# Modulation sums and narrow projections of a three-layer mixer network as fp32 products on column tiles

## The chip, the cores and the metric

The kernel runs on one core of a Trainium2 chip. The metric is the device time of one launch in microseconds; before the change its median over three runs is 2794.69 us (2786.75 to 2796.12).

## What is computed

A sequence of 512 tokens with 1024 features passes through one block of a first kind and two blocks of a second kind, in fp32. Each block starts by turning one conditioning row `c` into six rows of 1024 numbers (shift, scale and gate, once for the mixer and once for the feed-forward network):

```python
c_act = jax.nn.silu(c)
mod = c_act @ w_ada[l] + b_ada[l]          # 1024 -> 6 * 1024
sh1, sc1, g1, sh2, sc2, g2 = split(mod, 6)
h = rmsnorm(x, gain) * (1.0 + sc1) + sh1
proj = h @ w_in[l]                         # wide, with some narrow parts at its end
x = x + g1 * (mixer(proj) @ w_out[l])
h = rmsnorm(x, gain2) * (1.0 + sc2) + sh2
x = x + g2 * ((silu(h @ w_gate) * (h @ w_up)) @ w_down)
```

In the first block the mixer joins dilated attention (8 heads) and a gated delta rule (8 heads). The delta rule takes two gate logits per head, which are 16 of the columns of `w_in`. In the second kind the mixer joins three gated linear attentions. One of them takes its decays from a projection of rank 2 x 16, which is 32 of the columns of `w_in`. The output is one more RMS norm.

## The kernel before

Activations lie with the features on the partitions: `h` is 8 tiles of 128 x 512. To keep fp32 accuracy at the speed of the `fp32r` type, every weight strip and every activation is split into a high and a low part (`split`, L103 on ScalarE and L104 on VectorE). Each product is then made three times (`mm3`, L123 to L125: high x high, high x low, low x high). A projection (`proj`) loads one strip of 1024 x 128 weights, splits it, and issues 8 x 3 products of 512 columns. A product whose operands are plain fp32 shows as two records in the trace.

The order of work is written out by hand. A list `Dense` holds the projections with a cost for each; the mixer's own chains (delta rule, attention) call `d.fill(us)` at points where TensorE (PE) would stand, and so many projections are issued there. A second list, `extra`, rides on it: each step of the projections' list calls `extra.fill(0.6)`, and the mixer calls it at some further points. `extra.need("gate")` forces it up to a mark ahead of the state recurrence, and `extra.rest()` runs what is left after it. Within this order the compiler's scheduler may issue an instruction earlier when its engine has nothing else ready. Each engine then runs its queue in order. All weight loads are issued by one queue, SP.

The late part of the first block's modulation (the last four of its six rows, eight groups of 512 numbers) is `extra` of the first mixer (`ada_list(0, range(2, 6))`, then `ada`). For each group eight tiles `araw` of 128 x 512 weights are loaded (L311, two buffers). VectorE multiplies each by a column of `c_act` and adds it into `acc` (L313, L315), so that `acc` holds 128 partial sums per number. `ada_sum` adds up the partitions with one product whose weights are a single column (L333), ScalarE copies the row out (L334), and a DMA stores it in DRAM (`mods`, L335). `ada_load` and `ada_rows` bring the rows back as columns (a load, a transpose at L348, a VectorE add). A mark (`self.mark`, with `issue_after`) keeps VectorE's adds behind certain instructions of the mixer.

The modulations of the second and third block are `extra` of the feed-forward networks of the blocks before them (`ada_list(1 or 2, range(6))`). The sums are alike, with loads of 1 MB. Each finished `acc` is split into high and low parts and added up by two `fp32r` products with one column. Their groups are summed one at a time.

Two narrow projections use `proj` with few columns. `gates` (in `mixer1`) has 16 columns and is transposed by four small products (L620). `lr_in` (in `mixer2`, once per layer) has 32, and `c_decay` multiplies its rows by `wal` (L1254).

The first groups of the first modulation (`ada_first`) already use products on column tiles: L395 has weights of 32 columns, in `cz` one real column beside zeros, and `tile_position` puts four of them side by side. `mrow` is the copied row (L406), and L409 turns it into columns by products whose moving operand is one column of ones.

Of the kernel before, what the change touches and what calls it, by code (L numbers as in the profile page):

```python
# [30 lines left out]
def cap(ap, off, dims):  # L31
    return bass.AP(ap.tensor, ap.offset + off, [list(ap.ap[0])] + [list(d) for d in dims])
# [37 lines left out]
class Net:  # L70
    def __init__(self, ctx, tc, A, out, dbg=None):
        self.stages = self.mark = None
# [60 lines left out]
    def proj(self, w, act, kn, n=P, zero=None, tag="mm"):  # L133

        W = self.strip(w, kn, n, zero)
        ps = (self.mm if tag == "mm" else self.mx)()
        for k in range(kn):
            self.mm3(ps[:n], (W[0][:, k], W[1][:, k]), act(k), k == 0, k == kn - 1)
        return ps

# [70 lines left out]
    def setup(self):  # L211
# [4 lines left out]
        nc.gpsimd.memset(self.one, 1.0)  # L216
        self.scr = cp.tile([P, 1], F32, name="scr")
        self.mean = cp.tile([P, 1], F32, name="mean")
        nc.gpsimd.memset(self.mean, 1.0 / D)
# [3 lines left out]
        nc.sync.dma_start(out=crow, in_=A["c"].rearrange("a (r f) -> (a r) f", f=P))  # L223
        self.ident = self.const("c_ident", [P, P])
        self.lm = cp.tile([P, 160], U8, name="lm")
        self.xd = self.dp.tile([2, P, 4 * T], F32, name="xd")
# [34 lines left out]
    def setup2(self):  # L261
# [27 lines left out]
        self.lb, self.olb = lb, olb  # L289

    def ada(self, li, g, part):

        nc = self.nc
        w = self.A["w_ada"][0] if li == 0 else self.A["w_ada_2"][li - 1]
        cs = self.cs[min(li, 1)]
        if part == 0:
            if self.sums:
                self.ada_sum()
            self.acc = self.wp.tile([P, T], F32, name="acc", tag="acc", bufs=2)
        acc = self.acc  # L300
        n = 4 if li else 2
        if li:
            raws = self.t8("araw")
            nc.sync.dma_start(out=raws, in_=w[n * part * P:n * (part + 1) * P, T * g:T * g + T].rearrange("(k p) f -> p k f", p=P))
        with self.tc.issue_after(self.mark.ins) if self.mark else nullcontext():
            for k in range(n * part, n * (part + 1)):
                if li:
                    raw = raws[:, k % n]
                else:
                    raw = self.wp.tile([P, T], F32, name="araw", tag="araw", bufs=2)  # L310
                    nc.sync.dma_start(out=raw, in_=w[k * P:(k + 1) * P, T * g:T * g + T])  # L311
                if k == 0:
                    nc.vector.tensor_scalar(out=acc, in0=raw, scalar1=cs[:, 0:1], scalar2=None, op0=ALU.mult)  # L313
                else:
                    nc.vector.scalar_tensor_tensor(out=acc, in0=raw, scalar=cs[:, k:k + 1], in1=acc,  # L315
                                                   op0=ALU.mult, op1=ALU.add)
        if n * (part + 1) == KT:
            parts = [acc]
            if li:
                t = self.t8("ada", F32R)  # L320
                parts = [t[:, 0], t[:, 1]]
                self.split(parts[0], parts[1], acc)
            self.sums.append((li, g, parts))
# [12 lines left out]

# [244 lines left out]
    def mixer1(self, extra, norm):  # L581
# [148 lines left out]
        def delta_pairs(t):  # L730
# [16 lines left out]
            for e in range(2):  # L747
                h = 2 * t + e
                nt = self.t2("nt")
                v.tensor_tensor(out=nt, in0=ps[0][e], in1=gbs[e], op=ALU.mult)  # L750
                nc.gpsimd.dma_start(out=nts[4 * h:4 * h + 4].rearrange("t (j i) -> j t i", j=P), in_=four(nt))
                last = v.tensor_tensor(out=four(noff[h // 4][:, h % 4]), in0=four(nt), in1=mask(off), op=ALU.mult)
                v.tensor_tensor(out=qkm[h // 4][:, h % 4], in0=ps[1][e], in1=gbs[e], op=ALU.mult)
            if t == 1:
                self.mark = last

# [164 lines left out]
        def attend(h):  # L921
# [19 lines left out]
            for i in range(4):  # L941
                w = (i + 1) * P
                self.mark = v.tensor_scalar(out=pr[:, i, :w], in0=pr[:, i, :w], scalar1=sm[:, 8 + i:9 + i], scalar2=None,
                                            op0=ALU.mult)
# [12 lines left out]
            if e == 1:  # L957
                o = self.t2("oa")
                self.mark = v.tensor_copy(out=back(o), in_=pv[t])
                self.split(y[0][0][:, t], y[0][1][:, t], o)  # L960
# [242 lines left out]
    def mixer2(self, l, norm):  # L1203
# [31 lines left out]
        def lr_in():  # L1235
            wal = self.t2("wal")
            nc.gpsimd.memset(wal[:32], 0.0)
            for n in range(2):
                nc.sync.dma_start(out=wal[16 * n:16 * n + 16, 256 * n:256 * n + 256], in_=A["w_alpha_2"][l, n])
            ps = self.proj(W[:, 5632:5664], H, KT, n=32)  # L1240
            lr = self.t2("lr")
            nc.scalar.copy(out=lr[:32], in_=ps[:32])
# [286 lines left out]

    def ada_list(self, li, groups):  # L1530
        d = Dense()
        for g in groups:
            n = 2 if li else 4
            for i in range(2 * n):
                d.add("ada", 1.8 / n, lambda g=g, i=i: self.ada(li, 2 * g + i // n, i % n))
                if g == 3 and i == 0:
                    d.add("gate", 0.4, lambda: self.ada_rows(li, groups[0], 3))
            if g in (2, 5):
                d.add("ada", 0.4, self.ada_sum)
                d.add("ada", 0.4, lambda g0=max(g - 2, groups[0]), g1=g + 1: self.ada_load(li, g0, g1))  # L1540
        d.add("ada", 0.4, lambda: self.ada_rows(li, 3, 6))
        return d

    def run(self):
# [10 lines left out]
        mods = lambda li, i: (self.gain[li][:, 8 * i:8 * i + 8], self.mod[li][:, 24 * i:24 * i + 8])  # L1555
        self.mixer1(self.ada_list(0, range(2, 6)), self.norm(*mods(0, 1)))
        self.ffn(0, A["w_gate"][0], A["w_up"][0], A["w_down"][0], self.between, gained=True, extra=self.ada_list(1, range(6)))
        each, final = self.final_parts()
        for l in range(2):
            self.mixer2(l, self.norm(*mods(1 + l, 1)))  # L1560
            wf = A["w_ffn_in_2"][l]
            self.ffn(1 + l, wf[:, :2816], wf[:, 2816:], A["w_ffn_out_2"][l], final if l else self.norm(*mods(2, 0)),
                     extra=None if l else self.ada_list(2, range(6)), each=each if l else None)
        for _ in self.stages:
# [63 lines left out]
```

## Time and profile before

| | |
|---|---|
| median of three runs | 2794.69 us |
| the profiled execution's own time | 2791.13 us |
| its span, first to last instruction | 2789.3 us |
| PE busy | 2713.4 us (97%) |
| DVE (VectorE) busy | 1717.7 us (62%) |
| ACT (ScalarE) busy | 1173.5 us (42%) |
| mean granted TensorE clock | 0.990 |

The first mixer lies from about 60 to 435 us after the span's start, the first feed-forward network from there to about 800. PE means TensorE's matmuls, PEld its weight loads, DVE VectorE, ACT ScalarE, POOL GpSimd, SP the queue of the loads. "L333" is line 333 of the kernel. A matmul's record includes the time in which its results run out of the array, so records overlap; distances from start to start show how fast they follow each other.

### The profile page before, as it was taken

The numbers are of one execution on the slowest core, as the hardware profiler recorded it, in microseconds if no ns is written. First come the engines' busy times: TensorE is split into PE (matmuls) and PEld (weight loads), VectorE is DVE, ScalarE is ACT, GpSimd is POOL, SyncE is SP. The second block draws the span as 40 slices with busy tenths as digits, with TensorE's granted clock in tenths as the row PEclk, the third lists the DMA queues.
The fourth block names the chain that finished last, engine by engine and source line by source line (L and its number), as shares of the span: only waits on it lengthen the run. The fifth ranks groups of instructions, "written<-read, shape, count | busy, mean of one in ns | idle before, by whom it ended". The sixth has DMA issues, their size and how long they took to land.

```text
span 2789.3 us, 42619 instructions
## 1 busy us (share of the span) xinstructions
PE 2713.4 (97%) x17518; PEld 2202.2 (79%) x17518; DVE 1717.7 (62%) x2690; ACT 1173.5 (42%) x1799; POOL 41.7 (1%) x79
## 2 busy tenths in 40 slices
PE   8999999999999999999999999989999999999998
PEld 4786678888887787887888888877877878888887
DVE  4777756747378777757466573567777665533334
ACT  4643334222255655445343232465554453422223
POOL 0011000000000000100000000000000000000000
PEclk8999999999999999999999999999999999999999
DMA  7454534646232222332446463322223334333332
GB/s 262 135 148 121 148 123 151 219 151 219 85 107 70 62 81 69 104 104 72 136 129 233 143 228 94 105 62 69 70 75 91 101 85 131 89 99 98 96 94 83
DMA packets 471314, 330.65 MB, mean 119 GB/s; under 512 B 15447, under 2 KB 426223, under 8 KB 469584
## 3 DMA queue, kind: packets, MB, share of 16 engines
q1 hardware_dynamic: 468176, 320.51, 37.9%
q0 software_dynamic: 2944, 7.43, 0.9%
q8 instruction: 137, 2.24, 0.3%
q14 instruction: 57, 0.47, 0.1%
HBM read 312.55 MB, written 13.24 MB: 117 GB/s over the span
## 4 chain that ended last, share of the span: by engine, by line
PE 84%; DVE 5%; ACT 5%; DMA 3%; issue 2%; SPq 1%; POOL 0%; DVEq 0%; ACTq 0%; POOLq 0%
PE mm L123 21%; PE mm L124 21%; PE mm L125 21%; PE mx L124 2%; PE mx L123 2%; PE mx L125 2%; PE mm L201 2%; PE mm L203 2%; PE mm L202 2%; DMA araw<-in_w_ada_dram 1%; PE mx L1120 1%; ACT whi L103 1%; PE mx L131 1%; DVE S L104 1%; DVE wlo L104 1%
## 5 line engine op out<-in xcount | busy, mean ns | idle before, releaser
L123 PE MATMUL mm<-hh,whi 128*128 128x512 f32 (+1 forms) x2248 | 864.9, 388 | 13.8 <-ACT hh L495 9.0
L103 ACT CAST whi<-raw 128x1024 fp32r<-128x1024 f32 (+2 forms) x451 | 438.8, 974 | 1042.6 <-PE mm L124 737.9
L124 PE MATMUL mm<-hl,whi 128*128 128x512 f32 (+1 forms) x2248 | 868.4, 387 | 1.7 <-DVE hl L496 1.2
L125 PE MATMUL mm<-hh,wlo 128*128 128x512 f32 (+1 forms) x2248 | 867.1, 386 | 0.0
L104 DVE TENSOR_TENSOR wlo<-raw,whi 128x1024 fp32r<-128x1024 f32 (+2 forms) x451 | 507.2, 1126 | 364.3 <-ACT whi L103 343.0
L123 PEld LDWEIGHTS mm<-hh,whi 128*128 128x128 f32 x2248 | 421.1, 189 | 108.8 <-ACT hh L495 12.8
L124 PEld LDWEIGHTS mm<-hl,whi 128*128 128x128 f32 x2248 | 424.0, 189 | 88.8 <-DVE hl L496 4.6
L125 PEld LDWEIGHTS mm<-hh,wlo 128*128 128x128 f32 x2248 | 424.1, 189 | 87.6 <-issue 3.8
L124 PE MATMUL mm<-hid,whi 128*128 128x512 f32 (+1 forms) x564 | 212.5, 377 | 0.0
L123 PE MATMUL mm<-hid,whi 128*128 128x512 f32 (+1 forms) x564 | 212.3, 376 | 0.0
L125 PE MATMUL mm<-hid,wlo 128*128 128x512 f32 (+1 forms) x564 | 211.9, 376 | 0.0
L500 DVE SCALAR_TENSOR_TENSOR x<-mm,mod,x 128x512 f32<-128x512 f32 (+1 forms) x116 | 80.4, 694 | 178.0 <-PE mm L125 176.5
L315 DVE SCALAR_TENSOR_TENSOR acc<-araw,cs,acc 128x512 f32<-128x512 f32 x224 | 167.9, 749 | 19.0 <-DMA araw<-in_w_ada_dram 14.4
L550 DVE TENSOR_TENSOR sg<-mm,sg 128x512 f32<-128x512 f32 x66 | 45.6, 690 | 147.9 <-PE mm L125 146.0
L1176 DVE TENSOR_TENSOR R<-R,tot 128x512 f32<-128x512 f32 x192 | 126.4, 685 | 6.6 <-PE mx L1141 5.1
L201 PE MATMUL mm<-whi,hh 128*128 128x256 f32 x448 | 129.5, 289 | 0.0
L203 PE MATMUL mm<-whi,hl 128*128 128x256 f32 x448 | 129.2, 288 | 0.0
L202 PE MATMUL mm<-wlo,hh 128*128 128x256 f32 x448 | 128.8, 287 | 0.1
L123 PEld LDWEIGHTS mm<-hid,whi 128*128 128x128 f32 x564 | 106.1, 188 | 20.4 <-issue 1.2
L125 PEld LDWEIGHTS mm<-hid,wlo 128*128 128x128 f32 x564 | 106.1, 188 | 19.2
L124 PEld LDWEIGHTS mm<-hid,whi 128*128 128x128 f32 x564 | 106.1, 188 | 19.2
L454 DVE RECIPROCAL rstd<-rstd 128x512 f32<-128x512 f32 x24 | 80.4, 3351 | 13.4 <-ACT rstd L453 13.4
(377 smaller groups left out, 3375.7 us busy)
## 6 DMA issues: line engine op xcount, KB each, us to landing
raw<-in_w_in_dram SPq DMA_DIRECT2D x164, 512.0 KB
araw<-in_w_ada_dram SPq DMA_DIRECT2D x48, 1024.0 KB
raw<-in_w_ffn_in_dram SPq DMA_DIRECT2D x88, 512.0 KB
araw<-in_w_ada_dram SPq DMA_DIRECT2D x64, 256.0 KB
raw<-in_w_ffn_out_dram SPq DMA_DIRECT2D x32, 512.0 KB
raw<-in_w_gate_dram SPq DMA_DIRECT2D x22, 512.0 KB
raw<-in_w_up_dram SPq DMA_DIRECT2D x22, 512.0 KB
raw<-in_w_ada_dram SPq DMA_DIRECT2D x16, 512.0 KB
```

Of the source, the lines that this page charges most:

```text
L103: self.nc.scalar.copy(out=hi, in_=src)
L104: self.nc.vector.tensor_tensor(out=lo, in0=src, in1=hi.bitcast(F32), op=ALU.subtract)
L123: m(out=ps, lhsT=w[0], rhs=a[0], start=first, stop=False)
L124: m(out=ps, lhsT=w[0], rhs=a[1], start=False, stop=False)
L125: return m(out=ps, lhsT=w[1], rhs=a[0], start=False, stop=last)
L201: m(out=o, lhsT=a[0][:, sl], rhs=hi[:, k % 4], start=k == 0, stop=False)
L202: m(out=o, lhsT=a[0][:, sl], rhs=lo[:, k % 4], start=False, stop=False)
L203: m(out=o, lhsT=a[1][:, sl], rhs=hi[:, k % 4], start=False, stop=k == KT - 1)
L315: nc.vector.scalar_tensor_tensor(out=acc, in0=raw, scalar=cs[:, k:k + 1], in1=acc, op0=ALU.mult, op1=ALU.add)
L454: nc.vector.reciprocal(out=r, in_=r)
L500: self.nc.vector.scalar_tensor_tensor(out=self.x(f)[:, sl], in0=ps[:, sl], scalar=g[:, f:f + 1], in1=self.x(f)[:, sl], op0=ALU.mult, op1=A ...
L1176: v.tensor_tensor(out=o, in0=o, in1=half(1 - c), op=ALU.mult)
```

## The change

The late modulation of the first block is done in 16 steps, two for each group. A step (`ada_late`, `ada_raw`, `ada_mm`, `ada_cols`) loads four tiles of weights into four buffers and multiplies each by its column of `c_act`, repeated 32 times by a stride of 0. The four fp32 products stand side by side on the four column tiles. A step copies the result (128 x 512, four sums, each on 32 partitions) to `arow`. One step later it makes columns of it: four fp32 products with the moving column `four1`, which has ones at rows 0, 32, 64 and 96 and zeros elsewhere, and one add into `mod`. The rows no longer go through DRAM. The mark is gone.

The later modulations keep VectorE's sums. Up to four finished sums wait in one tile `accs` and are added up together, by fp32 products on four column tiles, without a split. Their rows are loaded and transposed once per block, not twice.

The narrow projections (`narrow`) use the unsplit weights: 16 fp32 products in four sets of four column tiles, each tile with a quarter of the contraction, for the high and the low part of `h`. The four partial results are added by the product that follows: in `gates` by a selecting matrix `sel`, in `lr_in` by four copies of `wal` on 128 rows.

```diff
+    def narrow(self, w, act):
+        raw = self.t2("wn")[:, :KT * 32].rearrange("p (k f) -> p k f", k=KT)
+        self.nc.sync.dma_start(out=raw, in_=w.rearrange("(k p) f -> p k f", p=P))
+        ps = self.mm()
+        for i in range(2):
+            for k in range(2):
+                for b in range(4):
+                    self.nc.tensor.matmul(out=ps[32 * b:32 * b + 32], lhsT=raw[:, 4 * k + b], rhs=act(4 * k + b)[i].bitcast(F32),
+                                          start=i + k == 0, stop=i + k == 2, tile_position=(0, 32 * b))
+        return ps
...
+    def ada_raw(self, g, part):
+        w = self.A["w_ada"][0]
+        raws = []
+        for k in range(4 * part, 4 * part + 4):
+            raws.append(self.wp.tile([P, T], F32, name="araw", tag="araw", bufs=4))
+            self.nc.sync.dma_start(out=raws[-1], in_=w[k * P:(k + 1) * P, T * g:T * g + T])
+        self.araw = raws
+
+    def ada_mm(self, part):
+        nc = self.nc
+        ps = self.mx()
+        for b in range(4):
+            nc.tensor.matmul(out=ps[32 * b:32 * b + 32], lhsT=cap(self.cs[0], 4 * part + b, [[0, 32]]), rhs=self.araw[b],
+                             start=True, stop=True, tile_position=(0, 32 * b))
+        self.arow = self.t2("arow")
+        nc.scalar.copy(out=self.arow, in_=ps)
+
+    def ada_cols(self, g, part):
+        nc = self.nc
+        pc = self.mx()
+        for j in range(4):
+            nc.tensor.matmul(out=pc[:, j:j + 1], lhsT=self.arow[:, j * P:(j + 1) * P], rhs=self.four1, start=True, stop=True)
+        c = slice(4 * g, 4 * g + 4)
+        mod = self.mod[0]
+        nc.vector.tensor_tensor(out=mod[:, c], in0=pc[:, :4], in1=(mod if part else self.V[0])[:, c], op=ALU.add)
+        if part and g == 9:
+            self.ada_gain(0, 4, slice(0, KT))
...
     def ada_sum(self):
...
-        li, g, parts = self.sums.pop()
         ps = self.mx()
         row = self.t2("row")
-        ones = self.mean128[:, 0:1] if li else self.mean
-        for i, a in enumerate(parts):
-            nc.tensor.matmul(out=ps[0:1], lhsT=ones, rhs=a, start=i == 0, stop=i == len(parts) - 1)
-        nc.scalar.mul(out=row[0:1], in_=ps[0:1], mul=float(P if li else D))
-        nc.sync.dma_start(out=self.mods[li][g:g + 1], in_=row[0:1])
+        n = len(self.sums)
+        for j, (li, g, acc) in enumerate(self.sums):
+            nc.tensor.matmul(out=ps[32 * j:32 * j + 32], lhsT=cap(self.one, 0, [[0, 32]]), rhs=acc, start=True, stop=True,
+                             tile_position=(0, 32 * j))
+        nc.scalar.copy(out=row[:32 * n], in_=ps[:32 * n])
+        for j, (li, g, acc) in enumerate(self.sums):
+            nc.sync.dma_start(out=self.mods[li][g:g + 1], in_=row[32 * j:32 * j + 1])
+        self.sums = []
...
         def gates():
-            ps = self.proj(W[:, 3584:3600], self.hact, KT, n=16)
+            ps = self.narrow(W[:, 3568:3600], self.hact)
             g = self.t2("g")
-            nc.scalar.copy(out=g[:16], in_=ps[:16])
+            nc.scalar.copy(out=g, in_=ps)
+            sel = consts[:, 448:464]
+            v.tensor_tensor(out=sel, in0=i64[:, 16:32], in1=i64[:, 48:64], op=ALU.add)
             pt = self.mx()
             for t in range(4):
-                nc.tensor.transpose(out=pt[:, 16 * t:16 * t + 16], in_=g[:16, t * P:(t + 1) * P], identity=self.ident[:16, :16])
+                nc.tensor.matmul(out=pt[:, 16 * t:16 * t + 16], lhsT=g[:, t * P:(t + 1) * P], rhs=sel, start=True, stop=True)
...
-            nc.gpsimd.memset(wal[:32], 0.0)
-            for n in range(2):
-                nc.sync.dma_start(out=wal[16 * n:16 * n + 16, 256 * n:256 * n + 256], in_=A["w_alpha_2"][l, n])
-            ps = self.proj(W[:, 5632:5664], H, KT, n=32)
+            nc.gpsimd.memset(wal, 0.0)
+            for b in range(4):
+                for n in range(2):
+                    nc.sync.dma_start(out=wal[32 * b + 16 * n:32 * b + 16 * n + 16, 256 * n:256 * n + 256],
+                                      in_=A["w_alpha_2"][l, n])
+            ps = self.narrow(W[:, 5632:5664], H)
...
-                    nc.tensor.matmul(out=ps, lhsT=st["wal"][:32, 256 * n + P * t:256 * n + P * t + P], rhs=st["lr"][:32],
+                    nc.tensor.matmul(out=ps, lhsT=st["wal"][:, 256 * n + P * t:256 * n + P * t + P], rhs=st["lr"],
                                      start=True, stop=True)
...
+    def ada_late(self):
+        d = Dense()
+        steps = [(g, part) for g in range(4, 12) for part in range(2)]
+        def step(i):
+            if i:
+                self.ada_cols(*steps[i - 1])
+            if i < len(steps):
+                self.ada_mm(steps[i][1])
+            if i + 1 < len(steps):
+                self.ada_raw(*steps[i + 1])
+        d.add("ada", 0.0, lambda: self.ada_raw(*steps[0]))
+        for i in range(len(steps) + 1):
+            d.add("gate" if i and steps[i - 1] == (5, 1) else "ada", 0.9, lambda i=i: step(i))
         return d
```

## Rows read from the trace of the kernel before

**Rows 1.** The page, busy microseconds by engine.

```profile
PE 2713.4 (97%) x17518; PEld 2202.2 (79%) x17518; DVE 1717.7 (62%) x2690; ACT 1173.5 (42%) x1799; POOL 41.7 (1%) x79
```

**Rows 2.** Busy time by stretch: its length; PE, PEld, DVE, ACT, POOL; clock; DMA.

```profile
75.00:180.00 105.00, 101.25 (x719) 86.85 (x720) 81.51 (x131) 67.60 (x98) 11.49 (x18) 0.95 0.50 149
180.00:330.00 150.00, 146.08 (x851) 104.17 (x850) 104.32 (x263) 56.06 (x130) 11.52 (x16) 1.00 0.46 131
330.00:372.00 42.00, 34.89 (x436) 25.74 (x434) 29.69 (x55) 8.94 (x18) 0.00 (x0) 0.96 0.66 204
...
440.00:800.00 360.00, 358.48 (x1620) 294.24 (x1618) 208.09 (x274) 117.51 (x158) 0.00 (x0) 1.00 0.51 163
```

**Rows 3.** Waits of PE from 75 to 440 us: in total, times, longest.

```profile
PE mx L333 <- DVE acc L315: 7.5, 4, 3.8
PE mx L685 <- ACT dsq L703: 3.2, 3, 1.7
```

**Rows 4.** The chain of waits from 75 to 440 us, by line.

```profile
by line: PE mm L123 9.4%; DMA araw<-in_w_ada_dram 9.4%; PE mm L124 9.3%; PE mm L125 9.0%; PE mx L955 5.2%; PE mx L932 4.6%; issue 4.3%; DVE acc L315 3.4%; PE mx L685 2.6%; PE mx L950 2.5%; PE mx L694 2.5%; DVE wlo L104 2.5%; DMA eg<-es 2.3%
```

**Rows 5.** Timeline of PE in the first feed-forward network: start, length, line, count.

```profile
512.55 0.63 PE L333 MATMUL mx<-ada,mean 128*1 128x512 f32 x2
513.02 0.39 PE L123 MATMUL mm<-hh,whi 128*128 128x512 f32 x1
513.25 0.39 PE L124 MATMUL mm<-hl,whi 128*128 128x512 f32 x1
```

**Rows 6.** Timeline of PE around one late modulation sum, in attention.

```profile
318.01 0.39 PE L124 MATMUL mm<-hl,whi 128*128 128x512 f32 x1
318.33 1.02 PE L333 MATMUL mx<-acc,mean 128*1 128x512 f32 x2
319.27 0.49 PE L817 MATMUL mx<-rr,yb 128*128 128x128 f32 x2
```

**Rows 7.** Timeline of PE around one transpose of modulation rows.

```profile
719.21 0.39 PE L125 MATMUL mm<-hh,wlo 128*128 128x512 f32 x1
719.53 0.24 PE L348 MATMUL mx<-c_ident,mrow 24*128 24x24 f32 x1
719.69 0.51 PE L123 MATMUL mm<-hh,whi 128*128 128x512 f32 x1
720.04 0.39 PE L124 MATMUL mm<-hl,whi 128*128 128x512 f32 x1
```

**Rows 8.** The group of one line and form, 60 to 420 us: busy, mean ns.

```profile
L315 DVE SCALAR_TENSOR_TENSOR acc<-araw,cs,acc 128x512 f32<-128x512 f32 x56 | 41.8, 747 | 14.5 <-DMA araw<-in_w_ada_dram 14.2
```

**Rows 9.** Timeline of PE in the first modulation groups (39 to 51 us).

```profile
39.81 1.05 PE L409 MATMUL mx<-one,mrow 128*128 128x1 f32 x8 [1.30 <-ACT mrow L406]
...
47.04 0.40 PE L124 MATMUL mm<-hl,whi 128*128 128x512 f32 x1
47.37 1.06 PE L395 MATMUL mx<-raw,cz 128*32 128x512 f32 x8
48.36 0.50 PE L125 MATMUL mm<-hh,wlo 128*128 128x512 f32 x1
48.70 0.40 PE L123 MATMUL mm<-hh,whi 128*128 128x512 f32 x1
...
49.41 0.94 PE L409 MATMUL mx<-one,mrow 128*128 128x1 f32 x8
50.28 1.24 PE L577 MATMUL mx<-hot 33*8 33x320 f32 x4
```

**Rows 10.** Timeline of PE at the gates' projection.

```profile
65.41 0.40 PE L123 MATMUL mm<-hh,whi 128*16 128x512 f32 x1 [1.19 <-ACT whi L103]
...
71.79 0.41 PE L620 MATMUL mx<-c_ident,g 16*128 16x16 f32 x4 [0.66 <-ACT g L617]
```

**Rows 11.** Waits of DVE, then of SP's queue, 60 to 420 us.

```profile
DVE acc L315 <- DMA araw<-in_w_ada_dram: 14.2, 19, 1.6
...
SPq L311 <- DVE acc L315: 79.5, 42, 10.8
```

More of the change, by code (lines that the diff above doesn't have):

```diff
@@ L71, in __init__ @@
     def __init__(self, ctx, tc, A, out, dbg=None):
-        self.stages = self.mark = None
+        self.stages = None
         self.sums = []
@@ L217, in setup @@
         self.scr = cp.tile([P, 1], F32, name="scr")
+        self.four1 = cp.tile([P, 1], F32, name="four1")
         self.mean = cp.tile([P, 1], F32, name="mean")
@@ L224, in setup @@
         self.ident = self.const("c_ident", [P, P])
+        for b in (32, 64, 96):
+            nc.vector.tensor_tensor(out=self.four1, in0=self.ident[:, 0:1] if b == 32 else self.four1,
+                                    in1=self.ident[:, b:b + 1], op=ALU.add)
         self.lm = cp.tile([P, 160], U8, name="lm")
@@ L293, in ada @@
         nc = self.nc
-        w = self.A["w_ada"][0] if li == 0 else self.A["w_ada_2"][li - 1]
-        cs = self.cs[min(li, 1)]
+        w = self.A["w_ada_2"][li - 1]
+        cs = self.cs[1]
         if part == 0:
-            if self.sums:
+            if len(self.sums) == 4:
                 self.ada_sum()
-            self.acc = self.wp.tile([P, T], F32, name="acc", tag="acc", bufs=2)
+            if not self.sums:
+                self.accs = self.t8("accs")
+            self.acc = self.accs[:, len(self.sums)]
@@ L300, in ada @@
         acc = self.acc
[L301 to L323, printed above, removed]
+        raws = self.t8("araw")
+        nc.sync.dma_start(out=raws, in_=w[4 * part * P:4 * (part + 1) * P, T * g:T * g + T].rearrange("(k p) f -> p k f", p=P))
+        for k in range(4 * part, 4 * part + 4):
+            raw = raws[:, k % 4]
+            if k == 0:
+                nc.vector.tensor_scalar(out=acc, in0=raw, scalar1=cs[:, 0:1], scalar2=None, op0=ALU.mult)
+            else:
+                nc.vector.scalar_tensor_tensor(out=acc, in0=raw, scalar=cs[:, k:k + 1], in1=acc, op0=ALU.mult, op1=ALU.add)
@@ L325, in ada_sum @@
+        if part == 1:
+            self.sums.append((li, g, acc))
     def ada_sum(self):
         nc = self.nc
-        li, g, parts = self.sums.pop()
         ps = self.mx()
         row = self.t2("row")
-        ones = self.mean128[:, 0:1] if li else self.mean
-        for i, a in enumerate(parts):
-            nc.tensor.matmul(out=ps[0:1], lhsT=ones, rhs=a, start=i == 0, stop=i == len(parts) - 1)
-        nc.scalar.mul(out=row[0:1], in_=ps[0:1], mul=float(P if li else D))
-        nc.sync.dma_start(out=self.mods[li][g:g + 1], in_=row[0:1])
+        n = len(self.sums)
@@ L751, in delta_pairs @@
                 nc.gpsimd.dma_start(out=nts[4 * h:4 * h + 4].rearrange("t (j i) -> j t i", j=P), in_=four(nt))
-                last = v.tensor_tensor(out=four(noff[h // 4][:, h % 4]), in0=four(nt), in1=mask(off), op=ALU.mult)
+                v.tensor_tensor(out=four(noff[h // 4][:, h % 4]), in0=four(nt), in1=mask(off), op=ALU.mult)
                 v.tensor_tensor(out=qkm[h // 4][:, h % 4], in0=ps[1][e], in1=gbs[e], op=ALU.mult)
-            if t == 1:
-                self.mark = last
         def q_decay(t):
@@ L942, in attend @@
                 w = (i + 1) * P
-                self.mark = v.tensor_scalar(out=pr[:, i, :w], in0=pr[:, i, :w], scalar1=sm[:, 8 + i:9 + i], scalar2=None,
+                v.tensor_scalar(out=pr[:, i, :w], in0=pr[:, i, :w], scalar1=sm[:, 8 + i:9 + i], scalar2=None,
                                             op0=ALU.mult)
@@ L958, in attend @@
                 o = self.t2("oa")
-                self.mark = v.tensor_copy(out=back(o), in_=pv[t])
+                v.tensor_copy(out=back(o), in_=pv[t])
                 self.split(y[0][0][:, t], y[0][1][:, t], o)
@@ L1236, in lr_in @@
             wal = self.t2("wal")
-            nc.gpsimd.memset(wal[:32], 0.0)
-            for n in range(2):
-                nc.sync.dma_start(out=wal[16 * n:16 * n + 16, 256 * n:256 * n + 256], in_=A["w_alpha_2"][l, n])
-            ps = self.proj(W[:, 5632:5664], H, KT, n=32)
+            nc.gpsimd.memset(wal, 0.0)
[4 more added lines that the diff above has]
+            ps = self.narrow(W[:, 5632:5664], H)
             lr = self.t2("lr")
-            nc.scalar.copy(out=lr[:32], in_=ps[:32])
+            nc.scalar.copy(out=lr, in_=ps)
             st["wal"], st["lr"] = wal, lr
@@ L1528, in regain, with ada_list @@
                                                 op0=ALU.mult, op1=ALU.mult)
-    def ada_list(self, li, groups):
+    def ada_list(self, li):
         d = Dense()
[L1532 to L1541, printed above, removed]
+        for g in range(12):
+            for i in range(2):
+                d.add("ada", 0.9, lambda g=g, i=i: self.ada(li, g, i))
+        d.add("ada", 0.4, self.ada_sum)
+        d.add("ada", 0.4, lambda: self.ada_load(li, 0, 6))
+        d.add("ada", 0.4, lambda: self.ada_rows(li, 0, 6))
+        return d
+    def ada_late(self):
[11 more added lines that the diff above has]
+            d.add("gate" if i and steps[i - 1] == (5, 1) else "ada", 0.9, lambda i=i: step(i))
         return d
@@ L1555, in run @@
         mods = lambda li, i: (self.gain[li][:, 8 * i:8 * i + 8], self.mod[li][:, 24 * i:24 * i + 8])
-        self.mixer1(self.ada_list(0, range(2, 6)), self.norm(*mods(0, 1)))
-        self.ffn(0, A["w_gate"][0], A["w_up"][0], A["w_down"][0], self.between, gained=True, extra=self.ada_list(1, range(6)))
+        self.mixer1(self.ada_late(), self.norm(*mods(0, 1)))
+        self.ffn(0, A["w_gate"][0], A["w_up"][0], A["w_down"][0], self.between, gained=True, extra=self.ada_list(1))
         each, final = self.final_parts()
@@ L1562, in run @@
             self.ffn(1 + l, wf[:, :2816], wf[:, 2816:], A["w_ffn_out_2"][l], final if l else self.norm(*mods(2, 0)),
-                     extra=None if l else self.ada_list(2, range(6)), each=each if l else None)
+                     extra=None if l else self.ada_list(2), each=each if l else None)
         for _ in self.stages:
```

## The prediction

> **What bounds the kernel now.** I began with the page's busy shares. TensorE (PE) is busy for 2713 of 2789 us, VectorE (DVE) for 62% of the span and ScalarE (ACT) for 42% [rows 1]. So a change counts by what it adds to or takes from PE, unless PE stands waiting where it acts. The busy time by stage says where it stands waiting [rows 2]: of 105 us in the delta part of the first mixer PE is idle 3.75, of the 150 us of attention 3.92, of the 42 us after it 7.11, and in the first feed-forward network 1.5 of 360. VectorE is never full, 104 of 150 us at most. What PE waits for there comes next: in the first mixer 7.5 us, four waits, are for the last sum `acc` of a modulation group (L315), and no other wait adds up to half of that [rows 3]. The chain of waits tempts to another reading: it lays 9.4% of this stretch on landings of `araw` and 3.4% on `acc`, 47 us of 365 [rows 4]. But a chain follows the last releaser, and PE had other work under most of it; what can be won is PE's idle time, not the chain's share.
>
> One more reading is needed. A matmul record of 0.39 us follows the one before it after 0.23 us [rows 5], so a record's length is no price. I take every price from start to start, with what the neighbours lose on both sides.
>
> **The change, part by part.**
>
> *Late modulation, removed.* Eight groups end in an fp32 product with one column (two records). Beside a sum in attention the starts read 318.01, 318.33, 319.27 [rows 6]: 0.09 lost ahead of it and 0.94 in it, 1.03 us; eight cost 8.2 us. The waits for `acc` go with them, 7.5 us [rows 3]. Two transposes of `mrow` go, each 0.32 - 0.23 + 0.16 + 0.12 = 0.37 by the one in the feed-forward network [rows 7], 0.7 us. Together 16.4 us of PE. Beside PE, 56 of the 64 multiply-adds alone free 41.8 us of VectorE [rows 8]. That is no term: VectorE wasn't the bound, and the work was hidden by PE's projections. SP loses eight `mods` stores and two `mrow` loads and keeps its 64 loads of `araw`.
>
> *Late modulation, added.* There are 16 steps. Each issues four fp32 products on the four column tiles, one ACT copy, four fp32 products with one moving column, and one small DVE add. The nearest row for the four products is the same form in the first groups: starts 47.04, 47.37, 48.36, 48.70 [rows 9]. From 47.04 to 48.70 are 1.66 us; the two neighbours need 2 x 0.23 of it, so a group costs 1.20 us and 16 cost 19.2. The four one-column products (eight records) take 0.87, from 49.41 to 50.28, and some 0.10 at the edge [rows 9]: 0.97 us, 15.5 for 16. Together 34.7 us on PE. The 16 ACT copies replace eight, on an engine with room (56 of 150 us, [rows 2]). They are hidden as long as a step's columns are made one step later, as the code writes it.
>
> The Trainium skill (TensorE: Matmul & The Clock Gate, "Measured speedup vs the span model") gives four row tiles 3.07 times the speed of one after another and column tiles about the same. By it a body would be 4 x 0.94 / 3.07 = 1.22 us (an estimate) where the row has 0.99. By the page the sum would be about 8 us higher over some 34 such sets. The row is this kernel's own form, and I take it.
>
> *Narrow projections.* Each of three (gates, and `lr` in two layers) drops 24 products of 0.23, 5.5 us, for 16 fp32 products in four sets; at the set's body of 0.99 [rows 9] and 0.21 at the edges 4.2 us, so 1.3 is saved. In `gates` the wait of 1.19 for the split weights goes too [rows 10], while four selecting products take the place of four small transposes: about 0.97 for 0.4. `gates` -1.9, the two `lr` -2.6. The 128-row `wal` products stream the same columns as before and cost the same. Six more `wal` DMAs per layer on SP, and a memset of four times the rows on POOL, are done ahead under the projections before `lr`; were that cover gone, the products with `wal` would wait for a landing, by the nearest row 1.6 us per layer [rows 11].
>
> *Later sums.* In two feed-forward networks 24 pairs of one-column products at 0.47 [rows 5], 11.3 us, become six sets of 1.20, 7.2 us: -4.1. Four transposes become two: -0.7. The splits of 24 sums leave ACT and DVE, hidden behind a full PE (358.5 of 360 us, [rows 2]).
>
> **The sum** on a full PE: 34.7 - 16.4 - 1.9 - 2.6 - 4.8 = +9.0 us. Against it stands what the added work can fill. The scheduler may put steps where PE stands still, since nothing orders them behind a mark any more. Outside the `acc` waits 14.8 - 7.5 = 7.3 us of idle are left from 75 to 372 [rows 2, 3]; I take half, 3.7 us, as a step of 1 to 2 us doesn't fit every gap. The granted clock averages 0.95 from 75 to 180 and 0.96 from 330 to 372 [rows 2]. It has two levels (1.2 and 2.4 GHz), so that is 10.5 and 3.4 us at the lower, worth up to 5.2 and 1.7 us of matmul time. The last is where PE waited longest for `acc`, 3.8 us [rows 3]. A fuller PE may get it back; I take 2 us in all. That leaves +9.0 - 3.7 - 2.0 = +3.3 us. The profiled execution is one of 2791.1 us, 1.8 of it outside the span, and 3.6 under the median of 2794.7 (three runs, 2786.8 to 2796.1). The difference holds for either, so I forecast the median: 2798.
>
> Three costs no row shows. An added step can make PE itself wait for `araw`: DVE waited for these loads 14.2 us in 19 times, 1.6 at the longest [rows 11]. Bounds are 0 per step (loaded a whole step ahead, four buffers) and 1.6 on each of 16, 26 us; I take 0, since a step's loads are issued as soon as the set before it is done and steps come some 10 us apart, but keep the other end. SP stood 79.5 us behind `acc` with an `araw` load at its head [rows 11]. Now it stands behind PE's set instead, with the weight loads queued behind it; between 0 and the same 1.6 us per step, and I take 0, as those strips are fetched several projections ahead. `arow` holds one of eight `t2` buffers between two steps, and the sets take 32 PSUM buffers where sums took 8. That can delay others by 0 to 0.66 us per step (the wait behind one copy from PSUM, [rows 10]); I take 0.
>
> **The rivals.**
>
> *Slower, by waits inside the steps.* Place: a step's columns or its set, on PE. In the first groups, where columns follow their copy at once, PE waited 1.30 us for the copied row at 39.81 [rows 9]. If steps come in bursts, the copy or the four loads aren't there in time, and PE, in order, stops all projections. Price: 16 x 0.66 to 1.30 (the lower is the wait behind the gates' copy, [rows 10]) on top of +9.0: +20 to +30, and 2814 to 2825 us. For it: the loads did come late for DVE. Against: the code leaves a step between, and the scheduler moves a set that isn't ready. It decides from 0.3 us per step, which lifts +3.3 past 8.4 us.
>
> *Faster, by the freed chain.* VectorE's part in the delta and state chains shortens by 41.8 us of queue [rows 8], PE's waits there vanish and the added steps fill what is left. Available are 7.3 us of idle, up to 6.9 of clock, and waits under 0.16 us that the records' length hides. It decides when more than 17.4 us of the 9.0 + 8.4 come back; at 20 the time is 2784. For it: the chain's 47 us [rows 4]. Against: a PE that is idle under 4% in 75 to 330.
>
> *The tiles overlap less than in the first groups.* In those the moving rows lay ready and the weights were zero-padded columns, here they are one column repeated. If the four run only two by two, a set's body is 2 x 0.94 where the row has 0.99, and 34 sets cost 30 us more: 2828. The row at 47.37 speaks against it [rows 9]. By the page's ratio, named above, the time would be 2806.
>
> *The edit does not do what it says* where the scheduler leaves sums or splits in place: the code has none left in these parts, so I give it nothing.
>
> **How the numbers follow.** The forecast +3.3 with its neighbours (all idle filled to none: -4 to +8): 0.45. Waits inside the steps: 0.27. Freed chain: 0.25. Less overlap: 0.03. A measurement of this kernel tells about 0.3%, 8.4 us, from no change. So faster 0.25, within 0.3% 0.45, slower 0.27 + 0.03 = 0.30. The range leaves out the upper part of the slow rivals and the far end of the fast one: 2780 to 2818. The likeliest case's own range is 2790 to 2803.
>
> **What would show it.** In the changed profile the 16 sets should stand at starts about 1.2 us apart from neighbour to neighbour less their own time, the columns at 0.9, and the waits of PE for `acc` gone. Idle of PE from 330 to 372 should fall from 7.1 to about 3. The first mixer should be longer by 8 to 12 us and each feed-forward network shorter by about 2.4. I am wrong if PE's list of waits has `araw` or `arow` with more than 5 us (then slower), or if the first mixer ends earlier than before (then faster).

## The result, and the profile after

The changed kernel takes 2808.18 us (median of four runs, 2805.86 to 2811.28), where the kernel before, run beside it, takes 2792.18 us (four runs, 2786.75 to 2796.12). The ratio is 1.0061, interval 1.0047 to 1.0076: 17 us, slower. The forecast was 2798, with a range of 2780 to 2818. The median lies in the range, but not in the likeliest case (2790 to 2803).

The page of the changed kernel, busy microseconds by engine:

```profile
span 2809.4 us, 42993 instructions
...
PE 2741.5 (98%) x17782; PEld 2218.5 (79%) x17782; DVE 1660.4 (59%) x2615; ACT 1155.9 (41%) x1762; POOL 42.1 (1%) x79
```

Against [rows 1], PE is busy for 28.1 us more and VectorE for 57.3 us less. The work did move from VectorE to PE, and the span followed PE: it is 20.1 us longer in these two executions.

Next the busy time by stretch (same columns as [rows 2]), then the waits of PE from 75 to 440 us (us in total, times, longest):

```profile
75.00:180.00 105.00, 100.12 (x691) 83.96 (x691) 70.88 (x116) 62.56 (x91) 10.77 (x17) 0.93 0.39 111
180.00:330.00 150.00, 150.00 (x818) 102.88 (x816) 79.47 (x228) 54.70 (x129) 12.49 (x16) 1.00 0.52 151
330.00:372.00 42.00, 41.64 (x451) 29.25 (x444) 16.35 (x40) 11.43 (x20) 0.00 (x0) 1.00 0.35 114
```

```profile
PE mx L729 <- ACT dsq L747: 3.9, 3, 2.7
PE mx L688 <- DVE gt L685: 0.6, 1, 0.6
PE mx L323 <- DMA araw<-in_w_ada_dram: 0.4, 1, 0.4
```

From 180 to 372 us PE's idle time fell from 11.0 us to 0.4, and the wait for `acc` [rows 3] is gone. From 75 to 180 it grew, from 3.75 to 4.88: the first set of the late modulation (L323) starts at 177 us, so this stretch got nothing to fill its gaps.

The groups of the new late modulation by line and form, 60 to 440 us (busy, mean ns, idle before):

```profile
L323 PE MATMUL mx<-araw,cs 128*32 128x512 f32 x128 | 28.0, 604 | 0.4 <-DMA araw<-in_w_ada_dram 0.4
L333 PE MATMUL mx<-four,arow 128*128 128x1 f32 x128 | 15.7, 244 | 0.0
L326 ACT COPY arow<-mx 128x512 f32<-128x512 f32 x16 | 9.4, 587 | 36.0 <-PE mx L323 36.0
```

The columns (L333) have 0.98 us a step (15.7 / 16), as forecast. The sets have 28.0 / 16 = 1.75 us, where a set whose four products stand together has a record of 1.06. PE's timeline shows why:

```profile
190.05 0.95 PE L333 MATMUL mx<-four,arow 128*128 128x1 f32 x8
190.93 1.06 PE L323 MATMUL mx<-araw,cs 128*32 128x512 f32 x8
191.93 0.50 PE L123 MATMUL mm<-hh,whi 128*128 128x512 f32 x1
...
228.21 0.86 PE L997 MATMUL mx<-pt,va 128*64 128x384 f32 x2
229.00 1.04 PE L323 MATMUL mx<-araw,cs 128*32 128x512 f32 x2
229.97 0.86 PE L997 MATMUL mx<-pt,va 128*64 128x256 f32 x4
230.77 1.06 PE L323 MATMUL mx<-araw,cs 128*32 128x512 f32 x6
231.76 0.50 PE L125 MATMUL mm<-hh,wlo 128*128 128x512 f32 x1
```

A product is two records. At 190.93 all four run in 1.00 us from start to start. At 229.00 one product of a set runs alone in 0.97 us. Then two products of attention (L997) follow, and the other three of the set take 0.99. The scheduler **tore** sets: the 16 stand in 26 pieces, and each piece costs a whole pass, whether it holds one product or four. 25 of them take 0.975 to 0.997 us, and one, whose two products start 0.57 us apart, takes 1.55.

### The profile page after: what moved, and what is told of

Same layout as the page of the kernel before. It is cut to its first block, busy times and chain, and to the rows that moved or that the text cites. A ratio compares the mean times of both kernels' runs of the same rounds, so it can differ in the third digit from the quotient of the medians.

```text
span 2809.4 us, 42993 instructions
## 1 busy us (share of the span) xinstructions
PE 2741.5 (98%) x17782; PEld 2218.5 (79%) x17782; DVE 1660.4 (59%) x2615; ACT 1155.9 (41%) x1762; POOL 42.1 (1%) x79
## 4 chain that ended last, share of the span: by engine, by line
PE 85%; DVE 5%; ACT 5%; issue 2%; DMA 2%; SPq 1%; POOL 0%; ACTq 0%; DVEq 0%
PE mm L123 21%; PE mm L124 21%; PE mm L125 21%; PE mx L124 2%; PE mx L123 2%; PE mx L125 2%; PE mm L216 2%; PE mm L214 2%; PE mm L215 2%; PE mx L1162 1%; PE mx L131 1%; ACT whi L103 1%; DVE wlo L104 1%; PE mx L323 1%; PE mx L997 1%
## 5 line engine op out<-in xcount | busy, mean ns | idle before, releaser
L125 PE MATMUL mm<-hh,wlo 128*128 128x512 f32 (+1 forms) x2224 | 858.5, 387 | 0.0
L359 DVE SCALAR_TENSOR_TENSOR accs<-araw,cs,accs 128x512 f32<-128x512 f32 x168 | 125.6, 750 | 6.2 <-DMA araw<-in_w_ada_dram 2.2
L214 PEld LDWEIGHTS mm<-whi,hh 128*128 128x128 f32 x448 | 88.0, 196 | 3.2 <-ACT whi L103 1.7
```

The costliest lines, as they stand in the source:

```text
L125: return m(out=ps, lhsT=w[1], rhs=a[0], start=False, stop=last)
L214: m(out=o, lhsT=a[0][:, sl], rhs=hi[:, k % 4], start=k == 0, stop=False)
```

## The experiments

Each is compared with runs of the kernel before on the same chip, so ratios are what can be compared between experiments: 0.001 is 2.8 us. Most intervals reach 0.001 to each side, so the difference of two ratios is known to some 4 us; those of the changed kernel, e1, e2 and e11 reach 0.0015, and differences with them are known to 5 or 6. Landmarks of single profiles differ by 3 us between kernels that do the same (attention starts at 198.8 us in the kernel before and at 202.2 in e4), so the ratios decide where the two disagree.

**e1, whole sets.** The changed kernel with the four products of a set kept together.

```diff
-        for b in range(4):
-            nc.tensor.matmul(out=ps[32 * b:32 * b + 32], ...)
+        last = None
+        for b in (3, 2, 1, 0):
+            with self.tc.high_priority(offset=URGENT) if last else nullcontext():
+                last = nc.tensor.matmul(out=ps[32 * b:32 * b + 32], ...)
```

> The changed kernel, but the four products of a late modulation set are issued next to each other in TensorE's order (the one whose load comes last goes first). Theory: in the profile of the changed kernel the 16 sets stand in 26 pieces, and each piece takes 0.98 us whether it holds one product or four, so ten pieces too many cost 10 x (0.98 + some 0.2 at the edges) = 12 us: about 2796 us where the changed kernel has 2808, 16 pieces of 1.0 us in the trace. Rival: the first mixer lost its time to the steps' other work (columns, copies, buffers), and the time stays at 2806 to 2810.

Measured 2804.06 us, ratio 1.0053 (1.0039 to 1.0068). All 16 sets are whole, at 0.995 us. But PE's waits, 75 to 440 us, have new lines:

```profile
PE mx L325 <- DMA araw<-in_w_ada_dram: 4.1, 2, 2.2
...
PE mx L994 <- DVE pr L987: 1.8, 1, 1.8
```

A set that must wait for its fourth load stops PE; a torn one starts with what has landed. The first mixer ends 6 us earlier, of ten single passes saved; the new waits are about as long as what is missing. By the medians the gain is 4 us, by the ratios 2: the interval holds the rival's times and not the theory's.

**e2, gates back.** The changed kernel with the gates by the wide projection again.

```diff
-            ps = self.narrow(W[:, 3568:3600], self.hact)
+            ps = self.proj(W[:, 3584:3600], self.hact, KT, n=16)
...
```

> The changed kernel, with the gates' projection and transposes as before. Theory: the narrow form of the gates gains nothing, since the next strip's split ends no earlier and TensorE then stands 3.0 us and falls to the lower clock for 10 us; the delta part began 3.7 us later than before. Undone, about 2804 us. Rival (the prediction's sum): it saves 1.9 us, and undoing it costs that, 2810 us.

Measured 2804.71 us, ratio 1.0057 (1.0043 to 1.0072). By medians that is 3.5 us better than the changed kernel, by ratios 1.1: too little to tell.

**e3, late modulation back.** The changed kernel with the first block's late modulation as before.

```diff
-        self.mixer1(self.ada_late(), self.norm(*mods(0, 1)))
+        self.mixer1(self.ada0_list(0, range(2, 6)), self.norm(*mods(0, 1)))
...
```

> The changed kernel, with the late modulation alone as before (VectorE's sums, one product per group, marks). Theory: the late modulation's steps cost the first mixer about 19 of its 23 us: about 2789 us, and the waits of TensorE for acc are back (about 7 us). Rival: the first mixer is longer because of the narrow gates and their clock, then 2800 or more.

Measured 2792.08 us, ratio 1.0007 (0.9997 to 1.0018). So the late modulation on PE costs 0.0054, 15 us (some 10 to 20 by the intervals), and the rest of the change together nothing that these runs can tell from zero.

**e4, later sums alone.** The kernel before with only the later sums four at once (`ada`, `ada_sum` and `ada_list` of the change for the second and third block).

> The kernel before, with the later sums alone four at once. Theory: TensorE is full in the feed-forward networks, so the 24 pairs of products that become six sets are worth 4.8 us there (2.4 in each): about 2787 us against 2792. Rival: the saving is taken up behind the next wait, and the time is that of before within 1 us.

Measured 2784.85 us, ratio 0.9979 (0.997 to 0.9988): 5.9 us faster. Between e4 and e3 stand only the narrow projections: they cost 0.0028, 8 us (some 4 to 12), where the forecast had them save 4.5. The next three runs look for that.

**e5, narrow gates alone** (e4 and the diff of e2 the other way round).

> The kernel before with the later sums four at once, and with the narrow form of the gates alone; to be set against 2784.9, the later sums alone. Theory: the narrow gates cost, since the first strip after them is cast on ScalarE behind the last activation of vd, which waits for VectorE; PE reaches that strip 3 us earlier and stands for as long, the granted clock falls with it, and the sum is about 3.5 us worse: 2788, with a wait of PE for whi of about 3 us near 68 and the lower clock for some 10 us after it. Rival, the price of the records alone (-1.9): 2783, and no such wait.

Measured 2791.72 us, ratio 1.0011 (1.0002 to 1.002): 9 us over e4, where the theory had 3.5. The order that the theory names is there, on ScalarE in front of the strip that PE waits for:

```profile
66.15 0.63 ACT L730 ACTIVATE vd<-vd 128x512 f32<-128x512 f32 x1 [2.45 <-DVE vd L728]
66.69 1.98 ACT L103 CAST whi<-raw 128x1024 fp32r<-128x1024 f32 x2
```

**e6, narrow `lr` alone** (e4 with the change's `lr_in`).

> The kernel before with the later sums four at once, and with the narrow form of lr in both later layers alone; against 2784.9. Theory: what PE saves in lr it then waits for kt, the decay chain behind it on ScalarE and VectorE, and the chain has got longer as lr is copied with 128 rows for 32 and wal comes by eight loads: PE waits over 5 us for kt in the second mixer, and the time is 2787 to 2789. Rival, the price of the records alone (-2.6): 2782, with the wait for kt as in the later sums alone.

Measured 2786.62 us, ratio 0.9995 (0.9987 to 1.0004): 4.5 us over e4, as the theory had it, but not for the reason that it gave. Apart, the two narrow forms cost 13 us, together 8 (e3 against e4), and the gates in the changed kernel 1 (e2). Each of these is known to some 4 to 6 us, and the prices need not add up. ScalarE's timeline in the first of the two later mixers:

```profile
816.38 1.28 ACT L1314 ACT_TABLE_LOAD   x1
817.68 1.06 ACT L1314 ACTIVATE la<-la 128x1024 f32<-128x1024 f32 x1
818.64 1.25 ACT L1310 ACTIVATE la<-mx,V 128x512 f32<-128x512 f32 x2
819.91 1.28 ACT L1316 ACT_TABLE_LOAD   x1
821.20 1.15 ACT L1316 ACTIVATE la<-la,one 128x1024 f32<-128x1024 f32 x1
822.37 1.28 ACT L1314 ACT_TABLE_LOAD   x1
823.67 1.06 ACT L1314 ACTIVATE la<-la 128x1024 f32<-128x1024 f32 x1
824.74 1.28 ACT L1316 ACT_TABLE_LOAD   x1
826.04 1.15 ACT L1316 ACTIVATE la<-la,one 128x1024 f32<-128x1024 f32 x1
827.21 1.28 ACT L1319 ACT_TABLE_LOAD   x1
```

The decay chain does an Exp (L1314) and a Ln (L1316) for each of two halves, and then Exp again. Here they alternate and cost five table loads, 1.28 us each. In the kernel before and in e4 this mixer has both Exp, then both Ln, and three loads; only the last mixer has five. In e4:

```profile
829.86 1.28 ACT L1298 ACT_TABLE_LOAD   x1
831.15 2.00 ACT L1298 ACTIVATE la<-la 128x1024 f32<-128x1024 f32 x2
833.17 1.28 ACT L1300 ACT_TABLE_LOAD   x1
834.47 2.19 ACT L1300 ACTIVATE la<-la,one 128x1024 f32<-128x1024 f32 x2
836.68 1.28 ACT L1303 ACT_TABLE_LOAD   x1
```

Every kernel with the narrow `lr` and no edge has five loads here (the changed one, e1, e2, e3, e6), every one with the wide `lr` three (the kernel before, e4, e5, e7, e8). The scheduler chose another order, presumably because the narrow `lr` feeds the chain at another moment. At the end of it PE waits for `kt`. In e6, 800 to 900 us:

```profile
PE mx L1171 <- ACT kt L1150: 5.4, 1, 5.4
```

The same wait is 0.3 us in e4, 1.1 in e5, e7 and e8, and 2.6 in the kernel before.

**e7, the strip after the gates cast ahead.** e5 with the weights that PE needs after the gates cast before the convolution of `vd`, not behind it: two order edges keep the convolution on VectorE and its activation on ScalarE behind that strip's split.

```diff
+            st["s1"] = self.strip(W[:, 1536 + P:1536 + 2 * P], KT, P, ahead=2 * URGENT)
+            st.pop("conv")(self.hi, self.lo)
             ps = self.narrow(W[:, 3568:3600], self.hact)
...
+                with self.tc.issue_after(hi.ins) if hi else nullcontext():
+                    nc.scalar.activation(out=dst, in_=dst, func=AF.Silu)
...
```

> As the narrow gates alone, with one thing more: the strip after the gates is loaded and cast ahead of the convolution of vd on VectorE and of its activation on ScalarE. Theory (the order on ScalarE and VectorE makes the wait): the 3 us wait for whi is gone, the granted clock stays up, and the time is 2783 to 2785, some 4 us below the narrow gates alone. Rival (the strip's load lands too late, or the four selecting products and the copy of 128 rows are what cost): the wait stays, for the load, or the gate chain is as late as before, and the time is 2787 to 2789.

Measured 2782.54 us, ratio 0.9979 (0.997 to 0.9988): 9 us under e5, and level with e4. The lines that tell: in e5 the wait of PE, and the busy time from 62 to 80 us with its clock (columns as in [rows 2]),

```profile
PE mm L123 <- ACT whi L103: 3.0, 1, 3.0
...
62.00:69.00 7.00, 3.96 (x30) 1.14 (x22) 3.50 (x5) 4.55 (x8) 0.00 (x0) 0.86 0.00 1
69.00:80.00 11.00, 10.97 (x35) 9.08 (x36) 4.15 (x11) 5.23 (x7) 0.00 (x0) 0.62 0.51 143
```

and the same in e7:

```profile
PE mx L676 <- ACT g L670: 4.3, 1, 4.3
...
62.00:69.00 7.00, 6.17 (x43) 2.50 (x41) 4.85 (x7) 4.44 (x6) 0.00 (x0) 1.00 0.08 19
69.00:80.00 11.00, 7.50 (x30) 6.29 (x31) 5.13 (x15) 7.85 (x11) 0.00 (x0) 0.84 0.59 180
```

The theory is half right. The wait for `whi` is gone and the time came back, but PE now waits 4.3 us for the copy of the gates, so the idle time by itself was not the price. The granted clock was a part of it: in e5 its mean of 0.86 and 0.62 makes 2.0 + 8.4, some 10 us at the lower level (1.2 of 2.4 GHz), in e7 and in e4 (1.00 and 0.84 there) 3.5. The difference is worth 3.4 us of matmul time. In e5 the delta part's first products (`dsq`) also start 50.2 us after the first projection, in e7 46.9, in the kernel before 46.3. The two overlap, so of the 9 us, which are known to some 4, about 5 stay unexplained. No run has the strip cast ahead beside the wide gates, so what the edge would be worth there is open.

**e8, a leaner late modulation.** Sets kept whole, both sets of a group adding up in one PSUM buffer, one copy and four columns a group; the narrow projections undone.

```diff
-                             start=True, stop=True, tile_position=(0, 32 * b))
+                                        rhs=self.araw[b], start=part == 0, stop=part == 1, tile_position=(0, 32 * b))
...
-            if i:
+            if i and steps[i - 1][1]:
                 self.ada_cols(*steps[i - 1])
```

> The late modulation on PE as changed, but with the four products of a set kept together, both sets of a group adding up in one PSUM buffer, and one copy and four columns per group in place of two; gates and lr by the wide projections, later sums four at once. Theory (what the late modulation costs is sets, tears and columns): 16 us as measured, less 4 for the tears and 8 x 0.97 = 7.8 for the columns, leaves 4 over the later sums alone: 2789. Rival: a PSUM buffer of the five is held over two steps, others wait for it, and the loads of araw still come late for whole sets: 2794 or more.

Measured 2793.21 us, ratio 1.0018 (1.001 to 1.0027), 11 us over e4: close to the rival. Of its two reasons the late loads are in the trace and a wait for PSUM buffers is not. PE's waits, 75 to 440 us, begin with

```profile
PE aps L327 <- DMA araw<-in_w_ada_dram: 5.5, 2, 4.0
```

Even with half the columns and no tear the late modulation costs PE more there than VectorE's sums did.

**e9 to e12, the orders mended.** An order edge puts both Exp ahead of both Ln on ScalarE:

```diff
-                nc.scalar.activation(out=a[:, r[t]], in_=a[:, r[t]], func=AF.Exp, scale=-1.0)
+                with self.tc.issue_after(last.ins):
+                    last = nc.scalar.activation(out=a[:, r[t]], in_=a[:, r[t]], func=AF.Exp, scale=-1.0)
```

and the same ahead of Ln. e9 is e4 with it:

> The kernel before with the later sums four at once (ratio 0.9979 to before), and in the decay chain both Exp put ahead of both Ln on ScalarE by an order edge. In the profiles of the wide lr ScalarE loads three tables for this chain in the first of the two later mixers and five in the second, at 1.28 us each. Theory (the kt wait is set by these loads): the second mixer's wait of PE for kt falls from 5.4 to about 2.8 us, and the ratio is 0.997, 2.6 us lower. Rival (another part of the chain sets it): no change, 0.998.

e10 is e6 with it:

> The narrow lr beside the later sums (ratio 0.9995 to before), with the same order edge in the decay chain. Theory: the narrow lr cost time since the scheduler's order gave the first later mixer five table loads in place of three; with three in both the waits for kt fall to about 3 us each and the ratio to 0.997 to 0.9975, 6 us lower, at least level with the ordered wide lr. Rival (the copy of 128 rows, the eight wal loads or the clock are what cost): 0.999 to 1.0.

e9 measured 2782.74 us, ratio 0.9974 (0.9966 to 0.9983); its wait for `kt` in the last mixer fell from 5.4 to 2.6 us, and the gain of 1.4 us by the ratios is within their uncertainty. e10 measured 2781.48 us, ratio 0.9971 (0.996 to 0.9982), 6.7 us under e6, as the theory had it. Its chain, ScalarE in the first of the two later mixers:

```profile
826.36 1.28 ACT L1315 ACT_TABLE_LOAD   x1
827.65 2.01 ACT L1315 ACTIVATE la<-la 128x1024 f32<-128x1024 f32 x2
829.68 1.28 ACT L1318 ACT_TABLE_LOAD   x1
830.97 2.19 ACT L1318 ACTIVATE la<-la,one 128x1024 f32<-128x1024 f32 x2
833.18 1.28 ACT L1321 ACT_TABLE_LOAD   x1
```

and PE's wait behind it:

```profile
PE mx L1171 <- ACT kt L1150: 2.6, 1, 2.6
```

Three loads for five, and a wait of 2.6 us for 5.4: two loads are 2.56 us. With the edge in both, the narrow `lr` (e10) lies 0.0003 under the wide one (e9); without it, it lay 0.0016 over it (e6 and e4). So the order on ScalarE, not the narrow `lr` itself, was its cost. The Trainium skill (ScalarE: Activation LUTs, "Table sets: the hidden batching unit") says to batch activations by table set, and this trace agrees, at 1.28 us a load. Its table puts Exp and Ln into one set, which would need no load between them; here each change between the two has one.

e11 puts the gains together (later sums, narrow gates with the strip ahead, narrow `lr` with the order; late modulation as before):

> Later sums four at once, narrow gates with the strip after them cast ahead, narrow lr with the ordered decay chain; late modulation as before. Theory (the narrow forms are no loss once the order on ScalarE is mended): ratio 0.996 to 0.9975, some 2779 to 2782 us for a before of 2789, the fastest of all. Rival (the narrow forms cost by themselves): 0.999 or more.

Measured 2777.42 us, ratio 0.9959 (0.9944 to 0.9974): 11 us faster than the kernel before and, by the ratios, 28 us faster than the changed one: the fastest of all, though e10 is within the uncertainty.

e12 is the changed kernel with both orders mended:

> The changed kernel (ratio 1.0061) with the two orders mended, nothing else. Theory: what is left is the late modulation's 16 us less the later sums' 6 and the narrow forms' small gain: 9 us of the gates and 5 of the decay chain go, ratio 1.001 to 1.002, some 2792 to 2795 us for a before of 2789. Rival (the waits only move, as PE is full in the first mixer by the added sets): 1.005 or more.

Measured 2800.46 us, ratio 1.0041 (1.0028 to 1.0053), between the two expectations: 5.6 us of the hoped-for 14 came back. In its profile the first products of attention start 6.6 us earlier than in the changed kernel (198.9 us), and at the end of the first mixer 2.1 us of that are left (445.4). The trace shows what came between: PE waits for `qa` until 258.49 us, and right behind that the granted clock falls. The wait and the stretch behind it in e12, and last the changed kernel's stretch 6.6 us later:

```profile
PE mm L123 <- ACT qa L963: 1.4, 1, 1.4
...
260.00:290.00 30.00, 30.00 (x170) 21.17 (x171) 10.96 (x37) 10.88 (x29) 2.99 (x4) 0.84 0.50 154
...
266.60:296.60 30.00, 30.00 (x192) 21.54 (x190) 12.01 (x38) 11.34 (x30) 3.00 (x4) 1.00 0.58 176
```

A mean of 0.84 over 30 us is 9.6 us at the lower level, worth 4.8; with the wait that is as much as was lost, 4.5 us, and more. In the two later mixers the wait for `kt` is 2.6 us each, in the changed kernel 5.4.

## Why the prediction was right or wrong

The range holds the measured time by luck: its upper part was kept for waits inside the steps, which did not come. The direction was right, +3.3 us forecast and +17 measured. By its own steps, in microseconds of ratio times 2790:

- **Late modulation removed (-16.4)**: its largest term is right, the waits for `acc` are gone with the sums. The others weren't measured by themselves.
- **Late modulation added (+34.7)**: the columns right (0.98 a step against 0.97), a whole set right (1.00 and an edge against 1.20), the number wrong. "A group costs 1.20 us and 16 cost 19.2" took it that four products issued together stay together. They stand in 26 pieces, ten passes more, some 10 us.
- **Absorption (-3.7)**: right in size. From 75 us to the end of the first mixer (the first product of the feed-forward network, at 424.4 us before and 447.5 after) PE is idle 18.9 us before (349.4 less 330.5 busy) and 7.8 after (372.5 less 364.7). That is 11.1 filled, 7.5 of it the waits for `acc` and 3.6 others. It came from 180 to 330 us (3.9 idle before, 0.8 of it for `acc`, and 0.0 after) and not from 75 to 180. The clock came back from 330 to 372 (0.96 to 1.00) and was lost around the gates: from 69 to 80 us it is 0.54, before 0.84.
- Late modulation in all: forecast +18.3 - 5.7 = 12.6, measured 15 (e3). That the two are so near is in part luck too: the ten passes too many would make it 23, and what took back some 8 us (e3's 15 is known to some 5) no run shows. The first mixer ends 23.1 us later in the two profiles, where 8 to 12 were named as the sign; some 4 of them are the gates' (first `dsq` product 50.1 us after the first projection, before 46.3). Tearing was dear, yet e1 shows that most of it wasn't had back by keeping sets whole: these wait for loads where torn ones begin with what has landed.
- **Narrow projections (-4.5)**: the step that failed, with +7.8 measured (e3 against e4). The prices of the records were right: the changed kernel's narrow `lr` stands at 839.81 and 841.55 with 1.74 us for eight products, 3.6 in all, where 4.2 was taken. What failed is "so 1.3 is saved", a saving counted on PE alone while PE goes on to wait for ScalarE, and with it "the wait of 1.19 for the split weights goes too": it went, and 3.0 us before the next strip came. The gates had no saving because that strip's cast stood behind an activation of `vd`, and the lower clock followed (e5, e7); it explains some 4 of the 9 us there. `lr` had none because ScalarE's order of Exp and Ln flipped (e6, e10). The prediction named the `wal` loads as the cover of `lr`, and not the chain that follows it.
- **Later sums (-4.8)**: right, -5.9 (-3.3 to -8.4). One set stands at 556.44 with its next neighbour at 557.43.

The sum: +3.3 forecast, +12.3 from the narrow projections, +2.5 from the late modulation, -1.1 from the later sums make +17. The measured parts are differences of the same ratios (changed kernel, e3, e4, before), so that they add up proves nothing.

The rivals. *Waits inside the steps* did not come in the changed kernel: 0.4 us for `araw`, none for `arow`. The reason given against it, that a set which isn't ready is moved, held, and the price of that moving is the tearing. Where sets were kept whole, the waits came (4.1 us in e1, 5.5 in e8). *The freed chain*: of 57 us less on VectorE no run shows that the span got anything beyond the idle time named above. *Less overlap*: a whole set takes 1.00 us for four products of 0.94 [rows 6], so a factor of 3.8. The Trainium skill's 3.07 for four row tiles (TensorE: Matmul & The Clock Gate, "Measured speedup vs the span model") is not seen here. A torn set has no overlap with what was put between.

## What to carry to other kernels

Products on column tiles are cheap only as long as they stand next to each other in PE's queue: count the pieces in the profile, not the sets in the code, and ask which load a set that is kept whole would wait for. Before a saving on a full engine is booked, look at what that engine does next: a strip's cast, an activation in front of it, a chain that ends in its next wait. An edit that moves the moment at which a chain is fed can flip the order in which a scheduler puts its parts, so compare the order on the other engines first; here the order edges were worth 9 us (e7 against e5) and 7 (e10 against e6), and the packing of the narrow projections itself nothing that can be told from zero (e7 against e4, e10 against e9). Beside the added sets of the changed kernel both edges gave 6 of the hoped-for 14 (e12), where a lower clock behind another wait stood against them.

## What was not expected of the hardware

One product on one of four column tiles takes as long (0.97 us at 229.00) as four that run together (1.00 at 190.93), and a product of another form between them ends the overlap. After PE had stood for 3.0 us before `whi` in e5, the granted clock was at the lower level for some 10 us; after 1.4 us before `qa` in e12 for 9.6; after 4.3 us in e7 for 3.5. In the kernel before, waits of 1.7 and 1.4 us in attention left it at 1.00 [rows 2]. What sets the difference no run shows.
